# One decoder layer on one core: the values' second and third column blocks, and the mixing's first two, as blocks with seven products in place of eight

## The chip, the core and the metric

The kernel runs on one core of one Trainium2 chip. The metric is device time in microseconds (us) of one execution. Three runs of the kernel before gave 2302.16, 2303.19 and 2305.45 us; the median, 2303.19 us, is what the changed kernel is measured against.

## The reference, cut to what matters

One layer works on 256 tokens of width 2048, all in float32: a gated feed-forward half (f1), two parallel token mixers, a second feed-forward half (f2), and a gated embedding. Two products of the mixers matter here:

```python
rq, rk, rv, rg, aq, ak, av, gate_r, gate_a = jnp.split(h @ w_in[i], SPLIT_POINTS, axis=-1)
...
ro = head_group_norm(retention_chunkwise(rq, rk, rv), ret_gn_g[i]).astype(h.dtype)
ret_branch = (jax.nn.silu(rg) * ro) @ w_ret_out[i]
...
mixed = (jax.nn.sigmoid(gate_r) * ret_branch + jax.nn.sigmoid(gate_a) * att_branch) @ w_mix_out[i]
h = layer_norm(alpha * h + mixed, ln_g[i, 1], ln_b[i, 1])
```

The **values** `rv` are 256 tokens by 2048 columns, from a 2048x2048 weight (`w_rv`). The **mixing** is the product with `w_mix_out` (`w_mix`), also 2048x2048. Both are cut into four blocks of 512 columns.

## The kernel before, in words

**One float32 product costs three matmuls.** Every operand is split into a high part, rounded to a format that TensorE takes at full rate, and a low part, the rest. `Sum.add` (L284 to L293) adds low x high (L291), high x high (L292) and high x low (L293) into one PSUM bank. A product here has a 128x128 stationary operand from the tokens and a 128x512 moving operand from the weights.

**The split is made on the chip.** A chunk of weights of 512 KB (128x1024) is loaded by SyncE into a raw tile, ScalarE casts it into the high part (L91), and VectorE subtracts to get the low part (L92). A chunk in the plain form is a `Single`. In a plain pair of units (`P`), two chunks serve two column blocks: 2 k-blocks x 2 token halves x 2 column blocks = 8 products, 24 matmuls.

**Seven products in place of eight.** A unit of kind `S` takes the same two chunks as a 2x2 by 2x2 product in Winograd's form of Strassen's scheme: 7 products, 21 matmuls. For that, `Seven.make` (L153 to L179) makes four sums of quarters of the weights on VectorE (L163 to L166) and splits four tiles (the raw chunk, one half of the other chunk, and the two tiles u and v of the sums). The token side needs such sums too: `forms_of` (L377) makes them for two pairs of k-blocks at once, with one addition that joins high and low (L374), four short sums (L362 to L365) and a split. At the end four banks that the products share, s0 to s3, are folded (`seven_common`, L392 to L399: one ScalarE copy, four VectorE additions), and four more additions (L1233) bring in the other four banks. `block` (L321) runs such a block: it needs eight PSUM banks, all that there are.

**What sets the order.** The order is written out by hand: the program is recorded line by line, and each engine does its instructions in that order. `plan` is the list of weight units in the order of use. `fill` (L184) loads units and makes their splits ahead of use, as far as `slots_for_weights` allows (a count of 4 KB slots out of 46) and as far as an amount of queued matmul time allows (`ahead` 45, `far` 90). It is called when a unit is done; VectorE and ScalarE get the split's instructions at that place in their queues. Small jobs, such as transposes and the retention of a head, stand in `side`, one per unit of weights.

**The stages around the change.** After the norm behind f1: block 0 of the values (bank `rv`), eight groups of rotary queries and keys (`rqk`, L980 to L983; each ends with a rotation, L906 to L913, in which VectorE joins two PSUM halves and shuffles them, and GpSimd does three multiplications or additions of 128x512, tiles `rr0` to `rr7`), then blocks 1, 2 and 3 of the values one after another (L988 to L991, two banks each, copied out at L966 and L967), then the retention's gates `rg`. Much later: the gates `ga` (two blocks with four units S each, L1236 to L1238, forms `gaf`), the attention's and retention's outputs `ma` and `mr` (two blocks with two units S each, forms `mrf`), and the mixing's four blocks `mo` (L1284 to L1306), the last of which runs into the norm. The transposed operand of the mixing, `mixt`, has eight tiles of two k-blocks. Tiles 4 to 7 come from the last block of `mr` and are transposed by side jobs (`turned`, L1247) during the first chunks of the mixing; the transposes of one tile use one PSUM bank `mxt`, which ScalarE and VectorE empty.

Of the kernel before, what the change touches and what calls it, by code (L numbers as in the profile page):

```python
# [12 lines left out]
ALU = mybir.AluOpType  # L13
# [9 lines left out]
ALPHA = 2.0**0.25  # L23
LN_EPS = 1e-5
GN_EPS = 1e-5
KD = D // P
# [22 lines left out]
def layer(ctx: ExitStack, tc: tile.TileContext, io):  # L49
    nc = tc.nc  # L50
    sync, act, dve, pool, pe = nc.sync, nc.scalar, nc.vector, nc.gpsimd, nc.tensor
# [11 lines left out]
    def banks(name):  # L63
        return [bank(name + str(j)) for j in range(2)]
# [152 lines left out]
    def slots_for_weights(n, ahead=45, far=90):  # L217
        room.update(slots=n, ahead=ahead, far=far)
# [84 lines left out]
    def tokens_out(key, n_k, lhs, ps, n=512, before=None):  # L303

        nk = 1024 // n
        sums = [Sum(ps[t][:, :n], n_k) for t in range(2)]
        for c in range(n_k // nk):
            u = take(key + (c,))
            tokens_chunk(u.chunk, c * nk, lhs, sums, (0, 1), range(nk))
            done(u)  # L310
            run_side()

    def block_units(units, keys):

        for kind, p in units:
            if kind == "P":
                plan.extend(Single(keys(n, p)) for n in range(2))
            else:
                plan.append(Seven(keys(0, p), keys(1, p)))

    def block(name, units, keys, lhs, forms, sums, fold, before=None):  # L321


        sevens = [p for kind, p in units if kind == "S"]
        if sevens:
            p1, p6, p7, q5 = (Sum(bank(f"{name}s{j}"), len(sevens)) for j in range(4))
        for j, (kind, p) in enumerate(units):
            if before is not None:
                before(j)
            if kind == "P":  # L330
                for n in range(2):
                    u = take(keys(n, p))
                    tokens_chunk(u.chunk, 2 * p, lhs, [sums[t][n] for t in range(2)], (0, 1))
                    done(u)
                    run_side()
                continue
            u = take(keys(0, p))
            a11, a12 = (half_of(lhs(2 * p + e), 0) for e in range(2))
# [12 lines left out]
            run_side()  # L351
            if p == sevens[-1]:
                fold(p1.ap, p6.ap, p7.ap, q5.ap)
# [23 lines left out]
    def forms_of(parts, name):  # L377
        hi, lo = (slot([P, 8, P], F32R, name + w) for w in "hl")
        return seven_forms(whole(parts, name + "w"), hi, lo)

    def units_of(order, sevens):

        sevens = list(sevens)
        plain = [p for p in range(KD // 2) if p not in sevens]
        return [(kind, (sevens if kind == "S" else plain).pop(0)) for kind in order]

    def block_sums(ps, units, n_k):

        s = sum(kind == "S" for kind, p in units)
        return [[Sum(ps[t][n], n_k - (2 * s if t and n else s)) for n in range(2)] for t in range(2)]  # L390

    def seven_common(p1, p6, p7, q5):  # L392

        e, w = slot([P, 2, 512], F32, "eve"), slot([P, 2, 512], F32, "evw")
        act.copy(e[:, 0], p1)
        dve.tensor_tensor(w[:, 0], e[:, 0], p6, ALU.add)
        dve.tensor_tensor(e[:, 1], w[:, 0], p7, ALU.add)
        dve.tensor_tensor(w[:, 0], q5, w[:, 0], ALU.subtract)
        dve.tensor_tensor(w[:, 1], q5, e[:, 1], ALU.subtract)  # L399
        return e, w  # L400
# [6 lines left out]
    def plan_tokens(key, n_k, nk=2):  # L407
        for c in range(n_k // nk):
            plan.append(Single(key + (c,)))
# [195 lines left out]
    def block_stats(stats, y, col):  # L605
        for t in range(2):
            dve.bn_stats(stats[:, t, col, :], y[col][:, t])

    def load_columns(src, col, name):
        v = slot([P, 2, 512], F32, f"{name}{col}")  # L610
        sync.dma_start(v, src[col])
        return v
# [4 lines left out]
    def load_for_norm(i):  # L617

        vectors.append(ln_vectors(i))
        if i < 2:  # L620
            p_raws.append(slot([P, 2, S], F32, "praw"))
            sync.dma_start(p_raws[0], io["pT"])
# [38 lines left out]
    ht = big.tile([P, KD, 512], F32R, tag="ht", name="xt")  # L661
# [255 lines left out]

    GATE_UNITS = units_of("PPSSPSSP", (0, 1, 2, 3))
    RET_UNITS = units_of("PPPSPSPP", (0, 1))
    gate_keys = lambda b: lambda n, p: ("w_in_f2", 29 + 4 * b + 2 * n, p)  # L920
    ret_keys = lambda b: lambda n, p: ("w_ret2", 4 * b + 2 * n, p)

    def plan_mixers():
        plan_tokens(("w_rv", 0), KD)
        for grp in range(8):
            plan_features([("w_in_f", grp)], KD)
        for blk in range(1, 4):
            plan_tokens(("w_rv", blk), KD)
        for grp in range(8, 16, 2):
            plan_tokens(("w_in_f2", grp), KD)  # L930
        plan_tokens(("w_av",), KD, nk=4)
        for grp in (20, 16, 17, 18, 19):
            plan_features([("w_in_f", grp)], KD)
        for grp in range(21, 29, 2):
            plan_tokens(("w_in_f2", grp), KD)
        for b in range(2):
            block_units(GATE_UNITS, gate_keys(b))
        for j in range(0, 8, 2):
            plan_tokens(("w_att2", j), KD // 2)
        for b in range(2):  # L940
            block_units(RET_UNITS, ret_keys(b))
        for blk in range(4):
            plan_tokens(("w_mix", blk), KD)

    def later(n, job):
# [5 lines left out]
    def mixers(ht, norm, residual, keepers, away):  # L951
        cos_r, sin_r, cos_a, sin_a = trig
        rhs = lambda k: (ht[:, k, :S], ht[:, k, S:])
# [8 lines left out]
        rv = []  # L962

        def values(blk, ps):
            v = slot([P, 2, 512], F32, f"rvs{blk}")
            act.copy(v[:, 0], ps[0])  # L966
            dve.tensor_copy(v[:, 1], ps[1])  # L967
            rv.append(v)

        ps = banks("rv0")  # L970
# [3 lines left out]
        for c in range(FRONT, KD // 2):  # L974
            u = take(("w_rv", 0, c))
# [4 lines left out]
        for grp in range(8):  # L980
            ps = banks(f"rqk{grp}")
# [3 lines left out]
        decay = [slot([P, 2, 384], F32, f"dec{j}") for j in range(4)]  # L985
        for j in range(4):
            act.dma_start(decay[j], io["decay"][:, 2 * j : 2 * j + 2, :])
        for blk in range(1, 4):  # L988
            ps = banks(f"rv{blk}")
            tokens_out(("w_rv", blk), KD, rhs, ps)  # L990
            values(blk, ps)  # L991

        ret_t = [None] * HR
        gate_v = [None] * HR
# [79 lines left out]
        for h in range(0, HR, 2):  # L1074
            ps = banks(f"rg{h}")
# [18 lines left out]
        ps = banks("av")  # L1094
# [111 lines left out]
        for grp in (18, 19):  # L1206
            attention_features(grp)

        made = {}
        forms = lambda p: made[p // 2](p % 2)  # L1210
        slots_for_weights(18)
        sig = []
        for j in range(4):
            def before(c, j=j):
                if c == 0 and j >= 2:
                    g = j - 2
                    made[g] = forms_of([ht[:, 4 * g : 4 * g + 4, :]], f"gaf{g}")

            ps = banks(f"gt{j}")
# [2 lines left out]
            for t in range(2):  # L1222
                act.copy(sig[-1][:, t], ps[t])
        assert not side

        def mixer_block(name, units, keys, lhs):

            ps = [banks(name + w) for w in "ab"]
            got = []
            block(name, units, keys, lhs, forms, block_sums(ps, units, KD), lambda *a: got.extend(seven_common(*a)))  # L1230
            for n in range(2):
                for t in range(2):
                    dve.tensor_tensor(got[n][:, t], got[n][:, t], ps[t][n], ALU.add)  # L1233
            return got

        slots_for_weights(22)  # L1236
        for b in range(2):
# [2 lines left out]
        mix_t = []  # L1240
        y = {}

        def of_pairs(v, k):
            a = v[k // 2][:, k % 2, :]
            return a[:, :S], a[:, S:]
# [11 lines left out]
        for j in range(4):  # L1257
            v = sig[4 + j]
# [21 lines left out]
            dve.scalar_tensor_tensor(sl, sl, ALPHA, p, ALU.mult, ALU.add)  # L1280

        lhs = lambda k: of_pairs(mix_t, k)
        slots_for_weights(16)
        for blk in range(3):  # L1284
            if blk == 2:
                load_for_norm(1)
            ps = banks(f"mo{blk}")
            y[blk] = load_columns(residual, blk, "mixy")
            tokens_out(("w_mix", blk), KD, lhs, ps)
            for t in range(2):  # L1290
                dve.scalar_tensor_tensor(y[blk][:, t], y[blk][:, t], ALPHA, ps[t], ALU.mult, ALU.add)
            block_stats(stats, y, blk)
        y[3] = load_columns(residual, 3, "mixy")
        ps = banks("mo3")
        sums = [[Sum(ps[t], KD)] for t in range(2)]
# [215 lines left out]
```

## Time and profile before

| what | number |
|---|---|
| median of three runs | 2303.19 us |
| the profiled execution's own time | 2305.66 us |
| its span, first to last instruction | 2303.6 us |
| mean granted TensorE clock | 0.995 |
| mean DMA rate | 202 GB/s |
| weight loads of the values and of the mixing | 32 each, 512 KB, 4.6 and 4.3 us to landing |

The profiled execution is one run, 2.5 us above the median of the others; 2.1 us of its time lie outside the span. In the page, a row of the second part has one digit for each fortieth of the span (57.6 us): the busy share of an engine in tenths. A row of a timeline has the start in us from the span's start, how long it took, engine, line, operation, the tile written, an arrow, the tiles read, and how many such instructions were merged; after it in brackets may stand the idle time before it and what ended that. Buffer and chunk numbers are left out of tile names: `lw_rv` is any low part of a chunk of `w_rv`. The prefix h is a high part, l a low part, r a raw tile, u and v the tiles of weight sums, b the split half chunk.

### The profile page before, as it was taken

Reading aid. Unit: us, or ns where it says so; the run is one execution under the profiler, and the core shown is the slowest. Engines: PE = TensorE matmul, PEld = TensorE weight load, DVE = VectorE, ACT = ScalarE, POOL = GpSimd, SP = SyncE. Lnnn points to the kernel's source line nnn. Section 1 sums busy time; section 2 is a strip of 40 time slices with the busy share of each in tenths; the row PEclk is TensorE's granted clock in tenths of the full one; section 3 lists DMA queues with packets and bytes.
Section 4 is the critical chain, followed back from the end, with each engine's and each line's share of the span. In section 5 each row is a group of like instructions: output and inputs, shape, how many; then the busy total and the mean of one; then the engine's idle time right before and its main releaser. Section 6 shows DMA issues by size and latency. Waiting matters only on the chain.

```text
span 2303.6 us, 28759 instructions
## 1 busy us (share of the span) xinstructions
PE 2271.7 (99%) x10466; PEld 1882.5 (82%) x10466; DVE 1945.0 (84%) x2467; ACT 1184.4 (51%) x1427; POOL 96.0 (4%) x53
## 2 busy tenths in 40 slices
PE   9999999999999999999999999999999999999997
PEld 7788888888887888888778888888888888888876
DVE  7999999988988774677789786779999999889876
ACT  5555555555553342435566454355565565655432
POOL 0000000000000430124000000000000000000000
PEclk9999999999999999999999999999999999999999
DMA  9566666665576665555447567576556566565771
GB/s 317 164 219 192 192 206 195 201 207 182 214 279 237 202 215 169 171 161 163 139 156 236 170 224 274 171 245 206 197 191 203 183 209 215 170 220 193 289 256 56
DMA packets 193725, 465.70 MB, mean 202 GB/s; under 512 B 14768, under 2 KB 16048, under 8 KB 193584
## 3 DMA queue, kind: packets, MB, share of 16 engines
q1 hardware_dynamic: 191456, 460.91, 60.8%
q10 hardware_dynamic: 2128, 2.97, 0.4%
q8 instruction: 82, 1.34, 0.2%
q14 instruction: 59, 0.48, 0.1%
HBM read 455.43 MB, written 8.39 MB: 201 GB/s over the span
## 4 chain that ended last, share of the span: by engine, by line
PE 95%; DVE 3%; DMA 1%; issue 0%; ACT 0%; SPq 0%; ACTq 0%; DVEq 0%
PE f2g L293 3%; PE f2g L291 3%; PE f2g L292 3%; PE f1g L291 3%; PE f1g L292 3%; PE f1g L293 3%; PE rqk L242 3%; PE f2u L292 2%; PE f2u L291 2%; PE f2u L293 2%; PE f1u L291 2%; PE f1u L293 2%; PE f1u L292 2%; PE aqk L242 2%; PE f2d L291 2%; PE f1d L291 2%
## 5 line engine op out<-in xcount | busy, mean ns | idle before, releaser
L92 DVE TENSOR_TENSOR lf_gu<-rf_gu,hf_gu 128x1024 fp32r<-128x1024 f32 (+1 forms) x283 | 334.2, 1213 | 9.6 <-ACT hf_gu L91 9.1
L91 ACT CAST hf_gu<-rf_gu 128x1024 fp32r<-128x1024 f32 (+1 forms) x283 | 282.1, 1045 | 19.4 <-DMA rf_gu<-in_f_gu 19.4
L92 DVE TENSOR_TENSOR lw_in_f<-rw_in_f,hw_in_f 128x1024 fp32r<-128x1024 f32 x140 | 195.6, 1427 | 29.3 <-ACT hw_in_f L91 27.1
L92 DVE TENSOR_TENSOR lf_down<-rf_down,hf_down 128x1024 fp32r<-128x1024 f32 x152 | 180.9, 1219 | 27.5 <-ACT hf_down L91 22.0
L91 ACT CAST hf_down<-rf_down 128x1024 fp32r<-128x1024 f32 x152 | 155.3, 1051 | 77.0 <-DMA rf_down<-in_f_down 27.0
L91 ACT CAST huf_gu<-uf_gu 128x1024 fp32r<-128x1024 f32 x70 | 73.7, 1053 | 159.2 <-DVE uf_gu L164 153.5
L91 ACT CAST hw_in_f<-rw_in_f 128x1024 fp32r<-128x1024 f32 x140 | 138.9, 1051 | 2.3 <-DMA rw_in_f<-in_w_in_f 2.0
L291 PE MATMUL f1g<-hf_gu,xt 128*128 128x512 f32 x247 | 97.2, 393 | 5.4 <-ACT hf_gu L91 5.4
L293 PE MATMUL f1g<-lf_gu,xt 128*128 128x512 f32 x247 | 96.8, 392 | 0.0
L292 PE MATMUL f1g<-hf_gu,xt 128*128 128x512 f32 x247 | 96.8, 392 | 0.0
L291 PE MATMUL f2g<-hf_gu,ht 128*128 128x512 f32 x247 | 96.5, 391 | 0.0
L293 PE MATMUL f2g<-lf_gu,ht 128*128 128x512 f32 x247 | 96.2, 389 | 0.0
L292 PE MATMUL f2g<-hf_gu,ht 128*128 128x512 f32 x247 | 96.1, 389 | 0.0
L91 ACT CAST hvf_gu<-vf_gu 128x1024 fp32r<-128x1024 f32 x70 | 73.8, 1054 | 29.4 <-DVE vf_gu L166 29.4
L816 ACT ACTIVATE eve<-eve 128x1024 f32<-128x1024 f32 x20 | 21.2, 1062 | 127.2 <-DVE eve L815 127.2
L92 DVE TENSOR_TENSOR luf_gu<-uf_gu,huf_gu 128x1024 fp32r<-128x1024 f32 x70 | 85.2, 1218 | 0.0
L92 DVE TENSOR_TENSOR lvf_gu<-vf_gu,hvf_gu 128x1024 fp32r<-128x1024 f32 x70 | 85.2, 1217 | 0.0
L291 PE MATMUL f2u<-hf_gu,ht 128*128 128x512 f32 x212 | 83.5, 394 | 0.0
L291 PE MATMUL f1u<-hf_gu,xt 128*128 128x512 f32 x212 | 83.3, 393 | 0.0
L292 PE MATMUL f2u<-hf_gu,ht 128*128 128x512 f32 x212 | 82.5, 389 | 0.0
L293 PE MATMUL f2u<-lf_gu,ht 128*128 128x512 f32 x212 | 82.5, 389 | 0.0
L292 PE MATMUL f1u<-hf_gu,xt 128*128 128x512 f32 x212 | 82.5, 389 | 0.0
(1333 smaller groups left out, 6433.7 us busy)
## 6 DMA issues: line engine op xcount, KB each, us to landing
rf_gu<-in_f_gu SPq DMA_DIRECT2D x351, 512.0 KB, 5.0
rf_down<-in_f_down SPq DMA_DIRECT2D x176, 512.0 KB, 4.5
rw_in_f<-in_w_in_f SPq DMA_DIRECT2D x148, 512.0 KB, 4.4
rw_rv<-in_w_rv SPq DMA_DIRECT2D x32, 512.0 KB, 4.6
rw_ret<-in_w_ret SPq DMA_DIRECT2D x32, 512.0 KB, 4.7
rw_mix<-in_w_mix SPq DMA_DIRECT2D x32, 512.0 KB, 4.3
rw_pg<-in_w_pg SPq DMA_DIRECT2D x32, 512.0 KB, 4.7
rw_att<-in_w_att SPq DMA_DIRECT2D x16, 512.0 KB, 5.3
```

Of the source, the lines that this page charges most:

```text
L91: act.copy(dst_hi, src)
L92: (lo_engine or dve).tensor_tensor(dst_lo, src, dst_hi, ALU.subtract)
L242: pe.matmul(ps[f], hi[:, kk, f * P : (f + 1) * P], rhs(k), start=k == 0, stop=k == n_k - 1,)
L291: pe.matmul(o, al, bh, start=first, stop=False)
L292: pe.matmul(o, ah, bh, start=False, stop=False)
L293: pe.matmul(o, ah, bl, start=False, stop=self.left == 0)
L816: act.activation(g, g, AF.Silu)
```

## The change

Blocks 1 and 2 of the values become one block of the kind of `ga`: eight pairs of chunks in the order P P S S P S S P, with the units S over k-block pairs 0 to 3. Its forms are made inside the block, in `before`: those of pairs 0 and 1 ahead of the first unit, those of pairs 2 and 3 ahead of the third. Block 3 stays as it was. The weight slots go to 24 ahead of the block and to 14 behind block 3. Blocks 0 and 1 of the mixing become one block in the order P P P S P S P P, with the units S over pairs 2 and 3; its forms (`mof`) are made ahead of the second unit. The residual's columns for the two blocks are loaded at its fifth and sixth units, and the weight slots go from 20 to 16 behind it in place of ahead. Blocks 2 and 3 of the mixing stay. `mixer_block` moves up and takes `before`.

```diff
+    MIX_UNITS = units_of("PPPSPSPP", (2, 3))
+    rv_keys = lambda n, p: ("w_rv", 1 + n, p)
+    mix_keys = lambda n, p: ("w_mix", n, p)
...
-        for blk in range(1, 4):
-            plan_tokens(("w_rv", blk), KD)
+        block_units(GATE_UNITS, rv_keys)
+        plan_tokens(("w_rv", 3), KD)
...
-        for blk in range(4):
+        block_units(MIX_UNITS, mix_keys)
+        for blk in (2, 3):
             plan_tokens(("w_mix", blk), KD)
...
-        for blk in range(1, 4):
-            ps = banks(f"rv{blk}")
-            tokens_out(("w_rv", blk), KD, rhs, ps)
-            values(blk, ps)
+        made = {}
+        forms = lambda p: made[p // 2](p % 2)
+
+        def mixer_block(name, units, keys, lhs, before=None):
+
+            ps = [banks(name + w) for w in "ab"]
+            got = []
+            block(name, units, keys, lhs, forms, block_sums(ps, units, KD), lambda *a: got.extend(seven_common(*a)), before)
+            for n in range(2):
+                for t in range(2):
+                    dve.tensor_tensor(got[n][:, t], got[n][:, t], ps[t][n], ALU.add)
+            return got
+
+        def before(u):
+            if u in (0, 2):
+                made[u // 2] = forms_of([ht[:, 2 * u : 2 * u + 4, :]], f"rvf{u}")
+
+        slots_for_weights(24)
+        rv += mixer_block("rv1", GATE_UNITS, rv_keys, rhs, before)
+        ps = banks("rv3")
+        tokens_out(("w_rv", 3), KD, rhs, ps)
+        values(3, ps)
+        slots_for_weights(14)
...
+        def before(u):
+            if u == 1:
+                made[1] = forms_of(mix_t[2:4], "mof")
+            if u in (4, 5):
+                y[u - 4] = load_columns(residual, u - 4, "mixy")
+
+        for n, v in enumerate(mixer_block("mo", MIX_UNITS, mix_keys, lhs, before)):
+            dve.scalar_tensor_tensor(y[n], y[n], ALPHA, v, ALU.mult, ALU.add)
+            block_stats(stats, y, n)
         slots_for_weights(16)
-        for blk in range(3):
-            if blk == 2:
-                load_for_norm(1)
-            ps = banks(f"mo{blk}")
-            y[blk] = load_columns(residual, blk, "mixy")
-            tokens_out(("w_mix", blk), KD, lhs, ps)
-            for t in range(2):
-                dve.scalar_tensor_tensor(y[blk][:, t], y[blk][:, t], ALPHA, ps[t], ALU.mult, ALU.add)
-            block_stats(stats, y, blk)
+        load_for_norm(1)
+        ps = banks("mo2")
+        y[2] = load_columns(residual, 2, "mixy")
+        tokens_out(("w_mix", 2), KD, lhs, ps)
+        for t in range(2):
+            dve.scalar_tensor_tensor(y[2][:, t], y[2][:, t], ALPHA, ps[t], ALU.mult, ALU.add)
+        block_stats(stats, y, 2)
```

In the recorded order of the changed kernel, TensorE has 18 matmuls fewer and VectorE 67 instructions more.

More of the change, by code (lines that the diff above doesn't have):

```diff
@@ L1207, in mixers @@
             attention_features(grp)
-        made = {}
-        forms = lambda p: made[p // 2](p % 2)
         slots_for_weights(18)
@@ L1224, in mixers @@
         assert not side
[L1226 to L1231, printed above, removed]
-                for t in range(2):
-                    dve.tensor_tensor(got[n][:, t], got[n][:, t], ps[t][n], ALU.add)
-            return got
         slots_for_weights(22)
@@ L1282, in mixers @@
         lhs = lambda k: of_pairs(mix_t, k)
-        slots_for_weights(16)
-        for blk in range(3):
-            if blk == 2:
-                load_for_norm(1)
-            ps = banks(f"mo{blk}")
-            y[blk] = load_columns(residual, blk, "mixy")
-            tokens_out(("w_mix", blk), KD, lhs, ps)
-            for t in range(2):
-                dve.scalar_tensor_tensor(y[blk][:, t], y[blk][:, t], ALPHA, ps[t], ALU.mult, ALU.add)
-            block_stats(stats, y, blk)
+        def before(u):
[6 more added lines that the diff above has]
+            block_stats(stats, y, n)
+        slots_for_weights(16)
+        load_for_norm(1)
[5 more added lines that the diff above has]
+        block_stats(stats, y, 2)
         y[3] = load_columns(residual, 3, "mixy")
```

## The prediction

> **What bounds the kernel now.** I read the page of the profile first, its busy rows, its slices and its chain; then the list of who waited for whom, TensorE's rows alone; then the rows of the stages that change.
>
> ```profile
> PE 2271.7 (99%) x10466; PEld 1882.5 (82%) x10466; DVE 1945.0 (84%) x2467; ACT 1184.4 (51%) x1427; POOL 96.0 (4%) x53
> ...
> PE   9999999999999999999999999999999999999997
> ...
> DVE  7999999988988774677789786779999999889876
> ...
> PEclk9999999999999999999999999999999999999999
> ...
> PE 95%; DVE 3%; DMA 1%; issue 0%; ACT 0%; SPq 0%; ACTq 0%; DVEq 0%
> ```
>
> TensorE is busy in every slice, at full clock, and holds 95% of the chain. A matmul taken away is worth its whole time, as long as TensorE does not wait for something else instead. VectorE is the next engine: 84% over the span, 9 tenths in the feed-forward halves, where units with seven products are already used.
>
> ```profile
> PE f1g L291 <- ACT hf_gu L91: 5.4, 1, 5.4
> PE lnps L509 <- DVE f1y L502: 5.3, 3, 4.8
> ...
> PE f11s L293 <- DVE luf_gu L92: 0.4, 1, 0.4
> ```
>
> TensorE's waits, ten lines in all, come to 17 us, nearly all at the start and at the norms. The last line shown is small, but it is the mechanism that matters here: a seven-product bank (`f11s`) waited for VectorE's low part of a sum of weights.
>
> **What a matmul is worth here.** The values' blocks 1 to 3 run from 835.39 to the first matmul of the gates `rg`.
>
> ```profile
> 835.39 0.39 PE L291 MATMUL rv<-hw_rv,ht 128*128 128x512 f32 x1
> ```
>
> ```profile
> L291 PE MATMUL rg<-hw_in_f,ht x128: 389/389/578, 900.7 to 1001.9; 128*128 128x512 f32 x128
> ```
>
> ```profile
> 835.40:900.70 65.30, 65.30 (x290) 54.06 (x289) 32.42 (x30) 25.84 (x30) 5.69 (x3) 1.00 0.69 225
> ```
>
> 3 blocks x 8 chunks x 12 = 288 matmuls in 65.31 us: 0.2268 us each, though a row says 0.39, because they overlap. The window's row gives VectorE 32.4 of 65.3 us here. A chunk is 12 matmuls, 2.72 us; a unit with seven products is 21, 4.76 us, where its plain pair has 24, 5.44 us.
>
> **Term 1, the matmuls removed.** 6 units x 3 = 18 matmuls, 12 in the values and 6 in the mixing: 12 x 0.2268 = 2.72 and 6 x 0.2268 = 1.36, together -4.08 us. This is all that can be gained; it is 0.18%.
>
> **Term 2, the values' vector work.** The same kind of block runs at 1184 to 1265 us (`ga`), and its rows price what a unit asks of VectorE.
>
> ```profile
> 1184.80 0.69 DVE L163 TENSOR_TENSOR uw_in_f<-rw_in_f,rw_in_f 128x512 f32<-128x512 f32 x1
> ...
> 1187.47 1.22 DVE L92 TENSOR_TENSOR lw_in_f<-rw_in_f,hw_in_f 128x1024 fp32r<-128x1024 f32 x1
> ...
> 1190.34 1.22 DVE L92 TENSOR_TENSOR lvw_in_f<-vw_in_f,hvw_in_f 128x1024 fp32r<-128x1024 f32 x1
> 1191.48 0.68 DVE L163 TENSOR_TENSOR uw_in_f<-rw_in_f,rw_in_f 128x512 f32<-128x512 f32 x1
> ...
> 1213.88 4.62 DVE L92 TENSOR_TENSOR lw_in_f<-rw_in_f,hw_in_f 128x1024 fp32r<-128x1024 f32 x4
> ```
>
> From one unit's first sum to the next unit's: 1191.48 - 1184.80 = 6.68 us of VectorE, against 4.76 of TensorE. A plain chunk costs VectorE (4.62 - 1.22) / 3 = 1.13 us against 2.72. In `ga` the first unit's sums are made in the stage ahead, so there is a lead to use up. A set of forms for the tokens is also made there, in the slack of the attention's stage:
>
> ```profile
> 1130.31 1.22 DVE L374 TENSOR_TENSOR gaf0w<-ht 128x1024 f32<-128x1024 f32 x1
> ...
> 1134.23 1.23 DVE L92 TENSOR_TENSOR gaf0l<-sums,gaf0h 128x1024 fp32r<-128x1024 f32 x1 [1.11 <-ACT gaf0h L91]
> 1135.37 1.22 DVE L92 TENSOR_TENSOR lw_in_f<-rw_in_f,hw_in_f 128x1024 fp32r<-128x1024 f32 x1
> ```
>
> A set takes 1135.37 - 1130.31 = 5.06 us of the vector queue, 1.1 of it spent waiting for ScalarE's cast. In the changed kernel's order, nothing of this is made early in the values: behind the last rotation's shuffle VectorE has, in this order, forms (5.06), units 0 and 1 (2 x 6.68), one plain chunk (1.13), forms (5.06), one plain chunk (1.13), units 2 and 3 (2 x 6.68). That is 39.1 us in a queue that is served strictly in order, so everything stands behind the forms. Its start and one more load on it:
>
> ```profile
> 825.47 0.76 DVE L909 STREAM_SHUFFLE rr6sh<-rr6v 128x512 f32<-128x512 f32 x1
> 826.11 7.93 DVE L92 TENSOR_TENSOR lw_rv<-rw_rv,hw_rv 128x1024 fp32r<-128x1024 f32 x4
> ...
> 836.62 0.73 DVE L909 STREAM_SHUFFLE rr7sh<-rr7v 128x512 f32<-128x512 f32 x1
> ```
>
> ```profile
> 826.37 2.12 POOL L911 TENSOR_TENSOR rr6v<-rr6v,trig 128x512 f32<-128x512 f32 x1 [4.60 <-DVE rr6sh L909]
> ...
> 830.80 2.15 POOL L913 TENSOR_TENSOR rk<-rr6v,rr6sh 128x512 f32<-128x512 f32 x1
> 837.43 1.29 POOL L911 TENSOR_TENSOR rr7v<-rr7v,trig 128x512 f32<-128x512 f32 x1 [4.47 <-DVE rr7sh L909]
> ```
>
> The shuffle at 825.47 is followed 0.64 us later, so the chain starts at 836.62 + 0.64 = 837.26. The second row is four plain splits that took 7.93 us where four took 4.62 in the row above: GpSimd's three instructions of the rotation ran beside them, and each held VectorE up by about 1.1 us, 3.31 in all. The rotation behind group 7 starts at 837.43 and now meets the forms, so I add 3.31 (bounds: 0, if the wait for the cast and the like take it up, to 3 x 1.29 = 3.87, the undisturbed length of such an instruction, in the last row). [...]
>
> How late is TensorE's last operand? The low part of v of unit 3: 837.26 + 39.1 + 3.3 = 879.7, and 0.1 for the last split's own end. What such a wait looks like:
>
> ```profile
> 83.92 1.22 DVE L92 TENSOR_TENSOR luf_gu<-uf_gu,huf_gu 128x1024 fp32r<-128x1024 f32 x1
> ```
>
> ```profile
> 85.20 0.50 PE L293 MATMUL f11s<-luf_gu,f1fh 128*128 128x512 f32 x1 [0.42 <-DVE luf_gu L92]
> 85.54 0.40 PE L291 MATMUL f11s<-hvf_gu,f1fl 128*128 128x512 f32 x1
> ```
>
> The matmul starts 0.06 us behind the split's end (83.92 + 1.22 = 85.14), and the next one 0.34 behind it in place of 0.23. So the last wait ends at about 879.8. Without any wait TensorE would be there, at the ninth matmul of unit 3, after 6 chunks, 3 units and 8 matmuls: 835.39 + 16.33 + 14.29 + 1.81 = 867.8. **It waits 12.0 us in all**, and 0.1 for the restart. The first wait is in unit 0, whose first low part is ready at 837.26 + 5.06 + 3.31 + 2.67 + 1.28 = 849.6, while TensorE wants it after 4 chunks and 2 matmuls, at 846.7. More follow in units 1 to 3 and at the second chunk of pair 6, which stands behind the second forms. Behind the last wait come 12 matmuls of unit 3, 24 of the last pair and 96 of block 3: 879.8 + 0.1 + 132 x 0.2268 = 909.9 to 910.1 for the start of `rg`, where it was 900.7. **The values: +9.4 us** (-2.72 + 12.1).
>
> What hides the rest:
>
> ```profile
> L91 ACT CAST hw_in_f<-rw_in_f 128x1024 fp32r<-128x1024 f32 x140 | 138.9, 1051 | 2.3 <-DMA rw_in_f<-in_w_in_f 2.0
> ...
> rw_rv<-in_w_rv SPq DMA_DIRECT2D x32, 512.0 KB, 4.6
> ```
>
> A unit's casts are three of 1.05 us and one of half that, under 3.7 us of ScalarE against VectorE's 6.68. The raw chunks of unit 2 are issued behind GpSimd's last instruction of the rotation (about 844) and land 4.6 us later, long before VectorE reads them at 866. The folds run under the last pair. Behind the block VectorE has 9 us of splits in block 3's 21.8, so the delay does not grow. The copies out of blocks 1 and 2 that go (4) were beside TensorE and gave nothing.
>
> **Term 3, the mixing.** Its template is the second block of `mr`, with the same order of units and the same side transposes.
>
> ```profile
> 1350.88 0.39 PE L291 MATMUL mr1a<-hw_ret,rett 128*128 128x512 f32 x1
> ...
> 1369.13 0.39 PE L291 MATMUL mr1s<-hw_ret,rett 128*128 128x512 f32 x1
> ...
> 1394.97 0.39 PE L291 MATMUL mo<-hw_mix,mixt 128*128 128x512 f32 x1
> ```
>
> ```profile
> 1368.34 0.68 DVE L92 TENSOR_TENSOR mixt<-mxt,mixt 128x512 fp32r<-128x512 f32 x1
> ...
> 1402.84 0.68 DVE L92 TENSOR_TENSOR mixt<-mxt,mixt 128x512 fp32r<-128x512 f32 x1
> 1403.44 1.22 DVE L92 TENSOR_TENSOR lw_mix<-rw_mix,hw_mix 128x1024 fp32r<-128x1024 f32 x1
> ```
>
> TensorE gets to the first seven-product unit 18.25 us into the block: 1394.97 + 18.25 = 1413.2. VectorE empties the first transposed tile at 1402.84, as before; behind it at 1403.4 stand the forms (5.06, to 1408.5), that unit's splits (6.68, to 1415.2), two transposed tiles (0.6 each), one plain chunk (1.13) and the last transposed tile, done 0.74 later at 1418.3. The unit's own operands come in time (its first low part at 1412.4, wanted at 1413.7). But its sixth product goes to the PSUM bank of the last transposed tile and must wait for that copy: due at 1413.2 + 5 x 0.68 = 1416.6, it starts at 1418.3, 1.7 us late and 0.1 for the restart. In `mr`, where the forms were made earlier, that copy was done at 1369.0 (the first row of the second fence), ahead of the sixth product at 1369.13 + 3.4 = 1372.5. The second unit starts later by that and finds its splits done. **The mixing: -1.36 + 1.84 = +0.5 us** (bounds -1.4 without the wait, +1.5 with a microsecond more of vector work). The residual additions behind the block are 5 us of VectorE beside block 2's first four chunks, whose splits are made ahead of them.
>
> **Sum.** +9.4 + 0.5 = +9.9 us. The profiled execution's 2305.66 (span 2303.6) would become 2315.5 (span 2313.4); on the median of 2303.19 that is **2313.0 us, +0.43%**. About 0.2%, 4.6 us, is what a measurement of this kernel can tell from no change.
>
> **Rivals.**
> 1. *GpSimd costs the chain nothing and the mixing does not wait.* Then 12.1 becomes 8.8 and the mixing gives -1.36: +6.1 - 1.4 = +4.7, 2307.9 us. For it: VectorE has 1.1 us of idle time in each set of forms into which a GpSimd instruction fits. Against it: the four splits above. Between this and the forecast all mixtures are possible. Chance 0.22.
> 2. *More is late than VectorE alone*: ScalarE's casts of the sums of unit 0 queue behind the forms' cast, or freed slots come late once TensorE waits, and each costs the chain a microsecond or two: +12 to +14, about 2316 us. For it: many vector instructions in the block wait for slots that TensorE must free. Against it: they wait for units that TensorE did at least one unit earlier. Chance 0.12.
> 3. *The other side: the vector work is hidden, as it is in `ga`.* No wait appears and the 18 matmuls are gained: -4.08, 2299.1 us, which a measurement could not tell from no change. It decides at the ninth matmul of unit 3: VectorE would have to be there by 867.8, so do in 30.5 us what the rows price at 42.4. For it:
>
> ```profile
> 1184.00:1265.00 81.00, 81.00 (x359) 67.03 (x358) 79.82 (x95) 52.38 (x59) 0.00 (x0) 1.00 0.66 217
> ```
>
> In `ga` VectorE has 79.8 us of work in 81.0, and TensorE's list has no wait there. Against it: `ga` starts with its forms made and a unit's lead, and the values start behind. A half-hidden chain, with under 8 us of waits, would end within 0.2%. Chance 0.06 with all that is half hidden.
>
> **Chances.** Forecast 0.60, rivals 0.22, 0.12, 0.06. The range takes in the forecast's bounds and most of rivals 1 and 2: 2307.8 to 2316.5. Slower by over 0.2%: all of the forecast and of rival 2, and most of rival 1, 0.88. Within 0.2%: the lower end of rival 1 and most of rival 3, 0.10. Faster: 0.02.
>
> **What would show each step right or wrong.** In the changed profile TensorE's list of waits should have new lines at the `rv1` banks for VectorE's `lw_rv`, `luw_rv`, `lvw_rv`, about 12 us together, first in unit 0; the first `rg` matmul should be near 910; VectorE should have no gap from 837 to 879 but the two waits for the forms' casts; the rotation's GpSimd instructions should take over 2 us each. In the mixing one wait of 1 to 2 us should stand at the fourth to sixth product of the first unit, for VectorE's `mixt`. The forecast is wrong if `rg` starts below 904, if the waits name ScalarE or DMA, or if the stages behind lengthen too.

## The result and the profile after

Four runs of the changed kernel gave a median of 2315.34 us (2314.49 to 2316.73), four of the kernel before 2303.77 us (2302.16 to 2305.45): a ratio of 1.0048, 95% interval 1.0033 to 1.0064. The change costs 11.6 us. The profiled execution after took 2314.91 us, its span 2313.1.

The page after, its busy rows, slices and chain:

```profile
PE 2270.3 (98%) x10448; PEld 1877.7 (81%) x10448; DVE 1991.9 (86%) x2534; ACT 1197.0 (52%) x1442; POOL 95.1 (4%) x53
...
PE   9999999999999989999999999999999999999997
...
DVE  7999999988988887777789788779999999889876
...
PE 93%; DVE 5%; DMA 1%; issue 1%; ACT 0%; DVEq 0%; ACTq 0%; SPq 0%
```

TensorE has 18 matmuls fewer, VectorE 67 instructions and 47 us more, and VectorE's share of the chain rose from 3% to 5%. The slices show little of it: one of TensorE's digits, the fifteenth (809.6 to 867.4 us), went from 9 to 8. The list of who waited for whom shows more (engine, tile and line that waited, what for; us in all, times, longest):

```profile
PE rv1s L293 <- DVE lw_rv L92: 6.5, 4, 2.5
...
PE lnps L509 <- DVE mixy L502: 2.8, 5, 1.1
...
PE rv1a L291 <- ACT hw_rv L91: 1.5, 1, 1.5
...
PE mos L291 <- DVE mixt L92: 1.3, 2, 0.7
...
PE rv1s L293 <- DVE luw_rv L92: 0.8, 1, 0.8
PE rv1a L293 <- DVE lw_rv L92: 0.7, 1, 0.7
```

Four lines at the `rv1` banks are new, 9.5 us together, and one at the mixing's `mos` banks. The stages give the sizes. In these rows of windows (start:end, length, then the busy us of PE, PEld, DVE, ACT and POOL, the clock, the DMA share, GB/s) each stage runs from its first matmul to the first one of the next, except the second, a stretch of 3.5 us inside the first. The profile after:

```profile
832.03:907.96 75.93, 66.39 (x278) 52.13 (x276) 61.90 (x72) 34.00 (x39) 4.86 (x3) 0.98 0.64 209
875.50:879.00 3.50, 3.50 (x9) 2.37 (x9) 3.50 (x4) 3.50 (x5) 0.00 (x0) 0.53 0.64 201
1402.26:1448.24 45.98, 44.71 (x204) 36.32 (x202) 43.05 (x51) 24.31 (x28) 0.00 (x0) 1.00 0.73 249
1448.24:1501.52 53.28, 51.35 (x233) 41.84 (x232) 42.47 (x57) 20.53 (x24) 0.00 (x0) 1.00 0.60 205
```

And the mixing in the profile before, its blocks 0 and 1 and then the rest with its norm:

```profile
1394.97:1440.42 45.45, 45.45 (x209) 37.61 (x208) 29.76 (x30) 21.96 (x24) 0.00 (x0) 1.00 0.77 260
1440.42:1491.70 51.28, 50.95 (x233) 41.94 (x232) 38.82 (x53) 18.42 (x22) 0.00 (x0) 1.00 0.54 166
```

The values (first row) take 75.93 us, where they took 65.29: **+10.6**. In the second row the granted clock is 0.53. The mixing's blocks 0 and 1 (third row) take 45.98 us, where before they took 45.45: **+0.5**. The rest of the mixing with its norm (fourth row) takes 53.28, where before it took 51.28: +2.0. The four stages between the values and the mixing agree within 0.02 us.

The stage ahead of block 0 of the values was 3.4 us shorter in the profile after, at the norm behind f1; it lies ahead of all that the change touches and differs by up to 3.6 us between the ten profiles, in no order that follows the edits. It goes with TensorE's clock: from 700 to 722 us the mean granted clock was 1.00 in the three profiles whose values begin earliest (717.5 to 717.7), the profile after among them, 0.92 in five (718.3 to 719.3), and 0.84 in the two latest (720.1 and 721.0), the profile before among them. That is why single times say little about half a per cent here, and why the experiments are read by stages as well as by medians.

### The profile page after: what moved, and what is told of

It reads as the page before. It is cut to its first block, busy times and chain, and to the rows that moved or that the text cites. A ratio compares the mean times of both kernels' runs of the same rounds, so it can differ in the third digit from the quotient of the medians.

```text
span 2313.1 us, 28832 instructions
## 1 busy us (share of the span) xinstructions
PE 2270.3 (98%) x10448; PEld 1877.7 (81%) x10448; DVE 1991.9 (86%) x2534; ACT 1197.0 (52%) x1442; POOL 95.1 (4%) x53
## 4 chain that ended last, share of the span: by engine, by line
PE 93%; DVE 5%; DMA 1%; issue 1%; ACT 0%; DVEq 0%; ACTq 0%; SPq 0%
PE f1g L291 3%; PE f1g L293 3%; PE f1g L292 3%; PE f2g L293 3%; PE f2g L291 3%; PE f2g L292 3%; PE rqk L242 3%; PE f1u L292 2%; PE f1u L291 2%; PE f1u L293 2%; PE f2u L291 2%; PE f2u L292 2%; PE f2u L293 2%; PE aqk L242 2%; PE f2d L293 2%; PE f1d L293 2%
## 5 line engine op out<-in xcount | busy, mean ns | idle before, releaser
L293 PE MATMUL f1u<-lf_gu,xt 128*128 128x512 f32 x212 | 82.6, 389 | 0.0
```

Of the source, the lines that this page charges most:

```text
L293: pe.matmul(o, ah, bl, start=False, stop=self.left == 0)
```

## The experiments

The theory is that of the prediction: TensorE waits for VectorE's queue, which has too much between the last rotation and the fourth seven-product unit, and GpSimd's instructions make that queue longer. The rivals: the loss comes from the mixing and its norm, or from ScalarE's casts and late slots.

| kernel | median us | ratio to before, 95% interval | values' stage us | mixing, blocks 0 and 1, us |
|---|---|---|---|---|
| before | 2303.77 | | 65.29 | 45.45 |
| after | 2315.34 | 1.0048 (1.0033 to 1.0064) | 75.93 | 45.98 |
| the values' part alone | 2312.92 | 1.0041 (1.0028 to 1.0053) | 76.01 | as before |
| the mixing's part alone | 2305.64 | 1.0005 (0.9996 to 1.0014) | 65.29 | 45.98 |
| values alone, forms early | 2306.65 | 1.0008 (1.0000 to 1.0017) | 66.54 | as before |
| values alone, rotation late | 2308.97 | 1.0020 (1.0011 to 1.0029) | 70.75 | as before |
| mixing alone, forms early | 2303.75 | 1.0001 (0.9992 to 1.0009) | 65.29 | 44.10 |
| values alone, both remedies | 2301.47 | 0.9992 (0.9983 to 1.0001) | 62.57 | as before |
| all, with the remedies | 2300.62 | 0.9983 (0.9974 to 0.9993) | 62.58 | 44.10 |
| after, once more | 2313.57 (one run) | | 74.63 | 45.97 |

The first four experiments were run beside a before of 2304.22 us, the last four beside one of 2303.74.

### The values' part alone

```diff
-        block_units(MIX_UNITS, mix_keys)
-        for blk in (2, 3):
+        for blk in range(4):
             plan_tokens(("w_mix", blk), KD)
```

with the mixing's loop over blocks as it was before.

> The values' part alone, the mixing as it was before. Theory (VectorE's queue is late: forms, locked by GpSimd, then four units): the stage from the first values' matmul behind rqk to the first rg matmul takes 75 to 76 us against 65.3, TensorE's waits in it 9 to 10 us plus restarts, the last lvw_rv split ends 41.3 us behind the first rvf0w addition; the whole +9.5 to +10.7 us against the kernel before. The clock rows will tell whether the half-clock stretch of 3.4 us behind the last wait belongs to the gaps (it comes again, 1.7 us) or to that execution. Rival (the mixing's half and the norm behind it bring most of the loss): under +8 us.

Measured: +8.7 us by the medians (the interval goes from +6.5 to +12.2; +9.5 to +10.7 was expected), +10.7 by the stage. The windows of the stage and of a stretch in it:

```profile
832.72:908.73 76.01, 66.36 (x278) 52.24 (x276) 61.89 (x72) 34.02 (x39) 4.86 (x3) 0.98 0.65 210
877.00:880.00 3.00, 2.94 (x7) 2.36 (x8) 3.00 (x4) 3.00 (x4) 0.00 (x0) 0.50 0.60 198
```

The half-clock stretch stands in the same place. TensorE is idle for 76.01 - 66.36 = 9.65 us, and the last split starts 41.3 us and ends 42.5 us behind the start of the first addition of the forms. The values' part carries nearly all of the loss; the mixing as the main cause is out.

### The mixing's part alone

```diff
-        block_units(GATE_UNITS, rv_keys)
-        plan_tokens(("w_rv", 3), KD)
+        for blk in range(1, 4):
+            plan_tokens(("w_rv", blk), KD)
```

with the values' loop over blocks as it was before.

> The mixing's part alone, the values as before. Theory: blocks 0 and 1 of mo take 46.0 us against 45.45 (-1.36 for six matmuls, +1.9 for two waits on mixt), and nothing behind them changes: +0.5 us. Rival 1 (the norm behind the mixing is late because of the change, as one profiled execution showed): +2.5 us, with 99 us from the first mo matmul to f2g in place of 96.7. Rival 2 (no wait for mixt): -1.4 us.

Measured: +1.4 us by the medians (the interval goes from -0.9 to +3.2), +0.5 by the stages. Its windows, the two blocks and then the rest up to the first matmul of f2, and its two waits on TensorE:

```profile
1391.65:1437.63 45.98, 44.70 (x204) 36.33 (x202) 43.04 (x51) 24.32 (x28) 0.00 (x0) 1.00 0.70 253
1437.63:1488.90 51.27, 50.94 (x233) 41.94 (x232) 42.51 (x57) 20.44 (x24) 0.00 (x0) 1.00 0.60 209
```

```profile
1412.72 0.50 PE L291 MATMUL mos<-huw_mix,mofl 128*128 128x512 f32 x1 [0.61 <-DVE mixt L92]
...
1415.05 0.50 PE L291 MATMUL mos<-hvw_mix,mofl 128*128 128x512 f32 x1 [0.68 <-DVE mixt L92]
```

The two waits are there, at the fourth and the sixth product of the first unit, and the rest takes 51.27 us as before: the norm is not late because of the change. What was late in the profile after is told by ScalarE's timeline there:

```profile
1480.49 1.05 ACT L91 CAST hf_gu<-rf_gu 128x1024 fp32r<-128x1024 f32 x1 [0.84 <-DMA rf_gu<-in_f_gu]
1485.02 1.05 ACT L91 CAST hf_gu<-rf_gu 128x1024 fp32r<-128x1024 f32 x1 [3.47 <-DMA rf_gu<-in_f_gu]
```

A cast for f2 waited 3.47 us for its weights, VectorE's split behind it came late, and behind that the norm's own work. In two other executions of the same mixing (this one and the changed kernel's second profile, below) that wait is missing, so the 2.0 us belong to that execution. It varies without the change too: in the four runs whose mixing is as before, it took 51.27, 51.80, 52.21 and 52.33 us.

### The values with their forms made early

```diff
         for grp in range(8):
+            if grp in (4, 6):
+                u = grp - 4
+                made[u // 2] = forms_of([ht[:, 2 * u : 2 * u + 4, :]], f"rvf{u}")
             ps = banks(f"rqk{grp}")
```

in place of the calls in `before`; the mixing as before.

> As the values' part alone, but both sets of token forms are made ahead of groups 4 and 6 of rqk, where VectorE has idle time. Theory (the queue decides): it is shorter by 2 x 5.06 = 10.1 us, ends at about the time TensorE wants the last operand (0 to 1.5 us late), so the stage takes 63 to 65 us and the whole is -2.7 to -1.2 us against before, if rqk does not lengthen. Rival (ScalarE's casts or slots that come free late are what TensorE waits for): the waits remain at 5 us or more and the whole is +3 us or more. Rival 2 (rqk has no room for the forms on VectorE): rqk's stage grows by 2 us or more.

Measured: +2.4 us, 66.54 us for the stage, rqk 0.27 longer. The direction is the theory's, 9.5 us less for the stage than in the values' part alone, but the forecast of a gain failed. Neither rival shows: TensorE's waits at the `rv1` banks come to 2.8 us, all of them for VectorE, and rqk hardly grew. VectorE's timeline shows where the gain was given back:

```profile
812.73 1.21 DVE L374 TENSOR_TENSOR rvf2w<-ht 128x1024 f32<-128x1024 f32 x1
813.97 1.40 DVE L362 TENSOR_TENSOR sums<-rvf2w 128x256 f32<-128x256 f32 x1
815.29 1.50 DVE L363 TENSOR_TENSOR sums<-rvf2w 128x256 f32<-128x256 f32 x1
...
821.00 4.62 DVE L92 TENSOR_TENSOR lw_in_f<-rw_in_f,hw_in_f 128x1024 fp32r<-128x1024 f32 x4
...
836.21 0.68 DVE L163 TENSOR_TENSOR uw_rv<-rw_rv,rw_rv 128x512 f32<-128x512 f32 x1
836.80 1.78 DVE L164 TENSOR_TENSOR uw_rv<-rw_rv 128x512 f32<-128x512 f32 x1
...
867.11 1.22 DVE L92 TENSOR_TENSOR lvw_rv<-vw_rv,hvw_rv 128x1024 fp32r<-128x1024 f32 x1
```

The second set stands right behind the shuffle of group 5, so GpSimd's rotation lengthens it to 821.00 - 812.73 = 8.3 us in place of 5.06. VectorE then enters the block late: unit 0's sums start 836.21 - 832.12 = 4.1 us behind the block's first matmul, where the forms started 1.8 us behind it in the profile after. From there the queue takes 32.1 us, 29.0 for the units and chunks and 3.1 for GpSimd's hold on unit 0's sums; its end, 36.2 us into the block, is 3.8 us too late. My expectation had asked only whether rqk itself would grow; it had not counted that VectorE could leave rqk late, nor that GpSimd's last rotation would then hold up unit 0's sums in place of the forms.

### The values with the last rotation late

```diff
     def rotate(ps, name, dst, cos, sin, shuffle):
-        q = joined(ps, name)
+        turn(joined(ps, name), name, dst, cos, sin, shuffle)
+
+    def turn(q, name, dst, cos, sin, shuffle):
...
             if u in (0, 2):
                 made[u // 2] = forms_of([ht[:, 2 * u : 2 * u + 4, :]], f"rvf{u}")
+            if u == 7:
+                turn(*last.pop())
```

Group 7 calls only `joined` at its old place, and GpSimd multiplies the shuffled half first, so that all three of its instructions wait for the shuffle.

> As the values' part alone, but the shuffle and the three GpSimd instructions of the last rotation come behind the fourth seven-product unit. Theory (GpSimd's instructions hold the short sums of the forms up): sums L362 to L364 take 0.42 us again in place of 1.4 to 1.5, the queue is 3.3 us shorter and starts 0.64 earlier, so the stage is 3.3 to 3.9 us shorter than in the values' part alone: the whole +5.5 to +7 us against before. Rival (the sums were slow for another reason, or the queue is not what decides): 0.6 us or less is gained.

Measured: +4.75 us by the medians, where +5.5 to +7 was expected, and +5.5 by the stage. VectorE's timeline of the forms and of the last split:

```profile
833.90 1.22 DVE L374 TENSOR_TENSOR rvf0w<-ht 128x1024 f32<-128x1024 f32 x1
835.15 0.43 DVE L362 TENSOR_TENSOR sums<-rvf0w 128x256 f32<-128x256 f32 x1
835.49 0.42 DVE L363 TENSOR_TENSOR sums<-rvf0w 128x256 f32<-128x256 f32 x1
835.83 0.42 DVE L364 TENSOR_TENSOR sums<-sums,rvf0w 128x256 f32<-128x256 f32 x1
...
872.01 1.22 DVE L92 TENSOR_TENSOR lvw_rv<-vw_rv,hvw_rv 128x1024 fp32r<-128x1024 f32 x1
```

The short sums take 0.42 us again. The last split ends 873.23 - 832.86 = 40.4 us into the block, where it ended 44.3 us into it in the values' part alone (875.79 + 1.22 - 832.72): 3.9 us less. Of these, 0.75 is the earlier start without the shuffle (1.04 us into the block in place of 1.79) and the rest GpSimd's hold. GpSimd's price is shown. The stage gained 5.3 us, more than the 3.3 to 3.9 expected and 1.4 more than the queue; that is the half clock, below.

### The mixing with its forms made early

```diff
-            if u == 1:
-                made[1] = forms_of(mix_t[2:4], "mof")
...
+            def before(u, b=b):
+                if b == 1 and u == 7:
+                    made[1] = forms_of(mix_t[2:4], "mof")
```

The new function goes to the second `mr` block; the values as before.

> The mixing's part alone, its forms made ahead of the last pair of the second mr block in place of ahead of the mixing's second unit. Theory (the wait on mixt comes from the forms and the first unit's sums standing ahead of the last transposed tile's copy): VectorE has 5.06 us less ahead of that copy, no wait on mixt is left, blocks 0 and 1 of mo take 44.1 us in place of 45.98 (before: 45.45), and the whole is -1.4 us against before. Rival (the sixth product waits for that bank whatever the vector queue does): the two waits stay, +0.5 us.

The window of the two blocks, and VectorE's copy of the last transposed tile:

```profile
1392.98:1437.08 44.10, 44.10 (x204) 36.48 (x202) 40.17 (x46) 23.49 (x27) 0.00 (x0) 1.00 0.73 272
```

```profile
1411.15 0.68 DVE L92 TENSOR_TENSOR mixt<-mxt,mixt 128x512 fp32r<-128x512 f32 x1
```

TensorE is busy for all of the 44.10 us: 1.35 less than before, the six matmuls. The copy ends 18.9 us into the block, where it ended 23.3 us into it in the profile after (1425.60 against 1402.26). By the medians nothing can be told from before (2303.75 against 2303.74, the interval from -1.8 to +2.1 us); the gain is shown by the stage alone.

### The values with both remedies

```diff
         for grp in range(8):
+            def before(c, u=grp - 1):
+                if c == 2 and u in (0, 2):
+                    made[u // 2] = forms_of([ht[:, 2 * u : 2 * u + 4, :]], f"rvf{u}")
+
             ps = banks(f"rqk{grp}")
-            features_out([(("w_in_f", grp), ps)], KD, both_halves)
+            features_out([(("w_in_f", grp), ps)], KD, both_halves, before)
```

and the late rotation as above; the mixing as before.

> The values' part alone with both remedies: the forms made ahead of the third chunk of rqk's groups 1 and 3, behind GpSimd's work on the rotation before, and the last rotation's shuffle and GpSimd instructions behind the fourth seven-product unit. Theory: VectorE starts on unit 0's sums at about 833.2 (on the scale of the values' part alone) and has 4 x 6.68 + 2 x 1.13 = 29.0 us to do, so it ends at 862 where TensorE wants the last operand at 864.5: no wait at the rv1 banks, the stage takes 62.6 us against 65.3, rqk stays at 89.4, and no half-clock stretch in the stage: -2.7 us. Rival (VectorE's queue is behind already when it enters the block, because rqk's splits and the rotations' locks fill it): waits of 1 us or more stay and the gain is 1.5 us or less.

The window of the stage, and VectorE's last split for it:

```profile
834.45:897.02 62.57, 62.57 (x277) 51.80 (x276) 52.10 (x60) 32.25 (x37) 5.65 (x3) 1.00 0.80 278
```

```profile
863.48 1.22 DVE L92 TENSOR_TENSOR lvw_rv<-vw_rv,hvw_rv 128x1024 fp32r<-128x1024 f32 x1
```

The split ends 30.25 us into the block, ahead of the 32.4 at which TensorE wants it; TensorE is busy throughout, the clock is whole, and the stage is 65.29 - 62.57 = 2.72 us shorter, the twelve matmuls to the hundredth. The medians give -2.3 us. Rqk kept its 89.4 us although its VectorE went from 68 to 75 busy us. Against the run with the forms early alone, two things changed together: the units' sums start 1.1 us into the block in place of 4.1, and GpSimd's hold of 3.1 is gone. Neither was run by itself; by these numbers each of the two alone would have left the last operand about 0.8 us late (an estimate: 36.2 - 3.0 - 32.4).

### All of it with the remedies

The values of the run before this one and the mixing with its forms early.

> The whole change with the remedies of the two runs before it. Theory: all 18 matmuls are gained, 18 x 0.2268 = 4.08: -4.1 us against before, 0.18%. Rival (what the parts gain is given back elsewhere, as the norm behind the mixing): -2 us or less of a gain.

Measured: 2300.62 us, -3.1 us by the medians; the ratio of 0.9983 (0.9974 to 0.9993) is -3.9 us, between -6.0 and -1.6. The windows of the values and of the mixing's two blocks have 62.58 and 44.10 us. Against before that is -2.7 and -1.35 us. This version beats both kernels, and the 18 matmuls are all there is in it.

### The changed kernel once more

The same kernel, no edit.

> The changed kernel once more. If the half-clock stretch belongs to the gaps, it comes again at 877 to 879 (0.427 us between matmuls, clock 0.7 in that window), and the stage takes 75.9 us again. If the late norm behind the mixing was that execution's transfers, mo to f2g takes 97.2 us (96.73 + 0.53) and not 99.27 again.

Its windows: the values, then four stretches inside them, the first and the third at a low clock:

```profile
833.63:908.26 74.63, 67.77 (x277) 53.60 (x276) 61.88 (x72) 33.91 (x39) 4.86 (x3) 0.95 0.66 213
847.00:851.00 4.00, 3.38 (x8) 2.70 (x9) 4.00 (x6) 2.04 (x3) 0.00 (x0) 0.58 0.28 60
851.00:864.00 13.00, 11.32 (x47) 8.39 (x46) 11.67 (x16) 5.97 (x7) 0.00 (x0) 1.00 0.46 144
864.00:868.00 4.00, 3.43 (x8) 2.73 (x9) 3.86 (x6) 2.25 (x4) 0.00 (x0) 0.59 0.79 256
868.00:908.00 40.00, 37.88 (x164) 30.40 (x163) 30.70 (x34) 18.73 (x22) 0.00 (x0) 1.00 0.71 227
```

The half clock did not come at the same place: two stretches, at 848 and 865, and none at 877. And yet the stage is 1.30 us **shorter** than in the profile after, with its one stretch. The reason is where they lie. VectorE's last split ends 44.29 us into the block in both (here 876.70 + 1.22 - 833.63). A slow TensorE ahead of that point waits less for it and loses nothing; behind it, each slow matmul is lost. From the end of that split to the first `rg` matmul there are 30.34 us here, 30.38 with the late rotation and 30.33 with the early forms, but 31.64 in the profile after and 31.72 in the values' part alone, the two with a stretch behind the last wait. So the 5.3 us of the late rotation are 3.9 of VectorE's queue and 1.3 of the half clock, which fell there between 859 and 864 (mean clock 0.66), ahead of the last wait. The mixing with its norm took 45.97 + 51.27 = 97.24 us, as expected if the late norm was that one execution's.

## Why the prediction was right

**The base (Term 1).** Eighteen matmuls at 0.2268 us. With the waits gone the values lose 2.72 us and the mixing 1.35 to 1.36: exact.

**The values' vector work (Term 2).** Forecast: from the first addition of the forms to the end of the last split 39.1 + 3.3 + 0.1 = 42.5 us. VectorE's timeline of the profile after:

```profile
833.82 1.21 DVE L374 TENSOR_TENSOR rvf0w<-ht 128x1024 f32<-128x1024 f32 x1
835.06 1.39 DVE L362 TENSOR_TENSOR sums<-rvf0w 128x256 f32<-128x256 f32 x1
836.37 1.51 DVE L363 TENSOR_TENSOR sums<-rvf0w 128x256 f32<-128x256 f32 x1
837.81 1.51 DVE L364 TENSOR_TENSOR sums<-sums,rvf0w 128x256 f32<-128x256 f32 x1
...
875.10 1.22 DVE L92 TENSOR_TENSOR lvw_rv<-vw_rv,hvw_rv 128x1024 fp32r<-128x1024 f32 x1
```

876.32 - 833.82 = 42.50 us, and VectorE had no gap but the two waits for the forms' casts (1.17 and 1.19). The rows of `ga`, priced one by one and added up in the order of the queue, gave it. That it agrees to the hundredth is luck: without GpSimd's hold the queue is 873.23 - 833.90 = 39.33 us in the run with the rotation late, where 39.2 was forecast, and the hold was a little less than forecast. GpSimd's share, forecast at 3.31 from splits of four times as many elements as these sums, was 4.41 - 1.27 = 3.14 (three sums here against the same three with the rotation late). The prediction's upper bound, 3.87, was too much. One sign that it named did not show: only the first of GpSimd's three instructions took over 2 us (2.08, then 1.47 and 1.35).

**The waits.** Forecast 12.0 us and 0.1. Against the stage without waits (62.57) the second profile of the changed kernel lost 12.06 us, the first 13.36; the values came to +9.3 and +10.6 for a forecast +9.4. The list of waits does not show the 12 us that the prediction had named as a sign: its lines at the `rv1` banks come to 9.5 and 6.9 us, because it counts idle time alone, and restarts and slow matmuls take up the rest. The lateness itself is as forecast: the matmul that needs the last operand starts 44.34 us into the block in both profiles and 32.43 us into it in the run with both remedies, 11.9 us later. The first wait, at unit 0, was forecast at 2.9 us and was 2.49 with about 0.3 for its restart. That the waits would slow the clock and that 1.3 us of it can fall behind the last wait was not foreseen; it is the largest term that the sum for this stage lacked.

**The mixing (Term 3).** Forecast +0.48, measured +0.53. The size and the place were right, the shape was not: one wait of 1.7 us at the sixth product was forecast, and there are two, of 0.61 and 0.67, with about 0.6 for their restarts, at the fourth and the sixth, since two transposed tiles, not one, were copied late. The sum held because the last copy sets it: forecast to end 1418.3 - 1394.97 = 23.3 us into the block, it ended 23.3 us into it, and what the first wait took the second no longer had to. Taking the forms away from ahead of the copies removed both.

**The rivals.** Rival 1 (GpSimd free) is out by the sums that took 1.4 to 1.5 us against 0.42; its argument, idle time in the forms, fails because GpSimd had finished at 839.0, ahead of VectorE's wait for the cast. Rival 2 (ScalarE or slots) has one line in the list, 1.5 us at `hw_rv`, and a wait that names ScalarE was among the signs of a wrong forecast. But that cast stands behind the forms' cast, for which ScalarE itself had been idle 5.9 us until VectorE's sums (L365) were done; and it did not lengthen the block, for VectorE's queue ended when the forecast had it end without that. Rival 3 (hidden) is out as the kernel stands, and its condition was right: with VectorE there ahead of the ninth matmul of unit 3, as in the run with both remedies, all waits go.

**The sum.** +9.9 us was forecast. By stages it is +9.9 in the second profile (9.34 + 0.52) and 13.2 in the first, with the 1.3 us of clock and the 2.0 us of a late transfer. The median's +11.6 lies between. The three runs of the changed kernel that were not profiled had a mean clock of 0.993, the profiled one 0.996: 0.003 of 2315 us is 6.9 us of clock, about four stretches of 3.41 us at half clock more (an estimate). Where these lay, and what part of the 1.7 us between +9.9 and +11.6 they are, stays open.

## What to carry to other kernels

A seven-product unit trades 0.68 us of TensorE for about 4.4 us more of VectorE (6.68 against two plain chunks of 1.13), so ask of the stage, not of the span, whether VectorE has a lead when the first unit starts. Write its queue down in order, with durations from a stage that already does the same, and compare its end with the time at which TensorE wants the last operand. What is moved out of the queue must be put where VectorE has idle time and GpSimd is quiet; the forms right behind a rotation left the last operand 3.8 us late, and ahead of a third chunk, with the rotation moved too, not at all.

## What the runs showed of the hardware

**Half clock after short gaps.** TensorE's timeline in the changed kernel's second profile:

```profile
847.62 0.80 PE L293 MATMUL rv1s<-lw_rv,ht 128*128 128x512 f32 x1 [2.49 <-DVE lw_rv L92]
848.22 0.63 PE L291 MATMUL rv1a<-hw_rv,ht 128*128 128x512 f32 x1
848.65 0.63 PE L292 MATMUL rv1a<-hw_rv,ht 128*128 128x512 f32 x1
```

One gap of 2.49 us was followed by matmuls 0.43 us apart for about 3 us, where 0.23 is the pace. In the first profile of the same kernel the same gap of 2.49 us was followed by none, and gaps of 1.62 and 0.77 us by a stretch. What differs shows when the stage is cut into windows of 3.41 us, the length of the first profile's stretch (875.74 to 879.15), laid so that one of them ends where a stretch begins. The windows ahead of the two stretches of the second profile:

```profile
844.21:847.62 3.41, 0.93 (x5) 0.42 (x3) 3.34 (x6) 2.14 (x3) 0.00 (x0) 1.00 0.92 375
861.28:864.69 3.41, 1.19 (x5) 0.42 (x4) 2.53 (x3) 3.26 (x4) 0.00 (x0) 1.00 0.63 196
```

And from the first profile the two windows on which the gap of 2.49 us falls, the window ahead of the stretch, and the stretch:

```profile
841.61:845.02 3.41, 1.92 (x9) 1.26 (x7) 3.34 (x6) 1.92 (x4) 0.00 (x0) 1.00 1.02 413
845.02:848.43 3.41, 2.41 (x11) 1.99 (x12) 3.41 (x4) 2.41 (x3) 0.00 (x0) 1.00 0.38 124
872.33:875.74 3.41, 1.47 (x5) 0.94 (x6) 3.41 (x4) 3.34 (x4) 0.00 (x0) 1.00 0.69 237
875.74:879.15 3.41, 3.41 (x9) 2.23 (x9) 3.41 (x4) 3.41 (x5) 0.00 (x0) 0.50 0.62 191
```

The windows ahead of the three stretches have 0.93, 1.19 and 1.47 us of matmuls in them; the two on which the gap of 2.49 us falls in the first profile have 1.92 and 2.41, and the clock is 1.00 in the windows behind them. The gap lay whole in one window in the second profile and was divided by a border in the first. The two stretches of the second profile begin 864.69 - 847.62 = 17.07 us apart, five times 3.41. In the profiles before and after as a whole, cut in the same way and the program's start and end aside, four windows at full clock were followed by half clock, with 0.26 and 1.62 us of matmuls (before, at 706.1 and 2201.2) and 1.47 and 1.29 (after, at 872.3 and 2213.8); the one with 1.56 (after, at 705.1) was not, nor was any of the others, which have 1.88 or more. No gap in the values' stage of either profile of the changed kernel was over 2.49 us, and the half clock came all the same. This is read from the traces; no run moved a gap against the windows, so what sets the half clock is not shown.

**Short vector instructions beside GpSimd.** Sums of 128x256 that take 0.42 us in the run with the rotation late, with no GpSimd instruction beside them, took 1.39 to 1.51 in the profile after, beside GpSimd instructions of 128x512. That is about 1.0 us each, on a quarter of the elements of the splits that lost 1.1 us each in the profile before, and sums of 128x512 went from 0.68 to 1.67 and 1.78 in the run with the forms early: the price did not follow the length of VectorE's instruction.

**Rounded parts and plain float32.** In the profile before, matmuls of 128x256 on rounded parts (L250) follow one another (1.12 - 0.28) / 7 = 0.12 us apart; one of 128x256 on plain float32 tiles (L1015) is recorded as two matmuls, and the next begins 0.43 us behind its start:

```profile
822.79 1.12 PE L250 MATMUL rqk<-ht,lw_in_f 128*128 128x256 f32 x8
...
1009.02 0.60 PE L1015 MATMUL ro<-rvs,rsc 128*128 128x256 f32 x2
1009.45 0.59 PE L1016 MATMUL ro<-rvs,rsc 128*128 128x256 f32 x2
```
